# Identity products written into the modelled waits of a hybrid two-layer step

## The chip, the cores and the metric

The kernel runs on one core of one Trainium2 chip. The metric is the device time of one execution in microseconds (us); the kernel before takes 2547.45 us, the median of 3 runs (2543.54 to 2550.54).

## The reference

One step of a streaming encoder with two layers. 512 new frames of one prompt stream and 16 frames of each of 8 running streams go through it: 640 rows of width 2048, as five token blocks of 128 rows. All arithmetic is in fp32.

```
for i in range(DEPTH):                      # 2 layers
    shift, scale, gate = split(c @ w_ada[i] + b_ada[i], 3)
    h = rmsnorm(x, norm_g[i]) * (1 + scale) + shift
    if i % 2 == 0:                          # layer 0: stick-breaking attention
        q, k, v, zg = split(h @ w_in, 4)    # 16 heads of 128
        A = exp(log_sigmoid(z) - sum of softplus(z) over the keys between)   # z = q k / sqrt(128)
        y = ((A @ v) * silu(zg)) @ w_out
    else:                                   # layer 1: gated linear attention (GLA)
        q, k, v, r, a = split(h @ w_in)     # 4 heads, 256 x 512 state
        S = exp(b_last) * S + (k * exp(b_last - b))^T v     # chunk by chunk
        y = (rmsnorm(o) * silu(r)) @ w_out
    x = x + gate * y
y = rmsnorm(x, final_norm_g)
```

The running streams also bring 512 cached keys and values each, and a GLA state that is read, updated and written.

## The kernel before, in words

**Stages.** The program is one stream of work, in this order on the span: a front stage of layer 0 (about 0 to 160 us: x is turned, the conditioning products with w_ada give shift and scale, and the first 512 columns of the input projection are made), the rest of the input projection, the attention of layer 0 together with its output projection (about 950 to 1500), the front of layer 1, its input projection with GLA beside it, the output projection of layer 1 and the final norm. Weights come from DRAM in pieces, are cast into a high and a low part (`wh`, `wl`, L134 on ScalarE (ACT) and L135 on VectorE (DVE)), and each product of the projections is three matmuls (high by high, high by low, low by high).

**TensorE's order.** The whole kernel runs with TensorE (PE) on a written order: PE executes its matmuls as the Python code issues them. The order of the other engines is made by a scheduler that simulates a timeline, save in a few stretches with a written order there too (a stretch from the end of the front stage of layer 0 on, and most of the front of layer 1). The Python code itself is a planner. It keeps a modelled clock, `pe["now"]`, which `by` moves on for each matmul (a high or low part of n columns: n/2400 + 0.0133 us; fp32: n/600 + 0.005 us; narrow ones by another rule) and `block` by 0.11 us for a 128-column transpose. The main matmuls are generators. Everything else that needs PE is a "lane", another generator, held by an object of class `Side`. A lane says with each `step` how long to wait on the modelled clock and which PSUM banks it will take. `tick` runs what is due, and `drive` runs main matmuls with a `tick` between them.

**Modelled waits.** At some places the main matmuls can't go on before a lane has come to some point (six in the front stage of layer 0 through `ready`, the groups of the output projections, the end of a stage through `finish`). There the planner calls `Side.until(done)`: while `done()` is false it calls `tick`, and if that ran nothing, it moves the modelled clock by 0.2 us. In before, such a step of 0.2 us emits nothing. It is a wait of the model alone; whether the chip waits at that place is decided by the semaphores of the instructions around it.

**What stands around those places.** In the front stage of layer 0 the lane `ada_mod` gets pieces `ar` of w_ada by DMA, 512 KB each for the earlier steps, and multiplies them with `cT` (L180, a product of 32 columns of weights in one of four column tiles, into the bank `z` or `tp`); L185 on DVE copies the sum to `ada_r`, L189 turns it by two identity products, and from it come shift and scale, and then the activations `h`. The main matmuls there are L516 (`six`: five banks `mm`, 512 columns of the projection for all tokens), 512 columns wide. After the stage come L592 (products of 320 columns). At the end of the attention stage PE turns cached keys (L1079, an identity product in fp32), makes scores of cached keys (L1093, L1098), the values (L1131), turns probabilities (L1116, L1117) and runs the output projection of layer 0 (L696). In the front of layer 1 the rows are turned (L1306, whose copy is ACT's L1308), L248 spreads the norm over all partitions by a product of `rstd_w` and the identity in fp32, and L516 again makes 512 columns. At the end of the GLA, L1853 multiplies the running streams' states `s`, which GpSimd's queue loads (`move`, L78), L1859 makes the new states' updates, L1591 turns outputs, L1628 makes decays, and L696 is now the output projection of layer 1.

**PSUM.** There are eight banks of 128 x 512 fp32. `share_banks` opens pools by tag: in both front stages 5 `mm`, 1 `z` and 2 `tp`; elsewhere other splits. `bank(tag)` hands out the next buffer of a tag; a write to it waits until the earlier user of the buffer has been read.

Of the kernel before, what the change touches and what calls it, by code (L numbers as in the profile page):

```python
# [8 lines left out]
F32 = mybir.dt.float32  # L9
# [6 lines left out]
P = 128  # L16
# [25 lines left out]
def hybrid_step_kernel(ctx: ExitStack, tc: tile.TileContext, A: dict, O: list):  # L42
# [9 lines left out]
    mm, turn_block = nc.tensor.matmul, nc.tensor.transpose  # L52
# [37 lines left out]

    psum = {}

    def share_banks(**bufs):

        banks.close()
        psum["pool"] = banks.enter_context(tc.tile_pool(name="ps", bufs=1, space=PS))
        psum["bufs"] = bufs

    def bank(tag):
        return psum["pool"].tile([P, 512], F32, tag=tag, name=f"ps_{tag}", bufs=psum["bufs"][tag])  # L100

    share_banks(mm=5, z=1, tp=2)


    ident = cp.tile([P, P], F32, name="ident")
# [55 lines left out]
    def ada_mod(pool, ring, i, j0, ns, tag, group, pace=None, close=None):  # L161
# [5 lines left out]
        for kt in range(0, KT, each * group):  # L167
            rs = []
            for k in range(kt, kt + each * group, each):
                r = ring()  # L170
                for e in range(each):
                    load(r[:, 4 * w * e:4 * w * e + 4 * w].rearrange("p (q m) -> p q m", q=2),
                         src[:, k + e, 0:2, 256 * j0:256 * j0 + 2 * w])
                rs.append(r.rearrange("p (e q c) -> p e q c", e=each, q=4))
            yield step(pace(group) if pace else 0.5, tiled=True)
            if acc is None:
                acc = bank(tag)
            for m in range(each * group):
                for q in range(4):
                    mm(acc[32 * q:32 * q + 32, :w], cT[:, kt + m, :], by(cT[:, kt + m, :], rs[m // each][:, m % each, q, :]),  # L180
                       start=kt + m == 0, stop=kt + m == KT - 1)
# [3 lines left out]
        dve.tensor_copy(row, acc[:, :w])  # L185
        yield step(1.5, tp=1)
        tp = bank("tp")
        for s in range(ns):
            turn_block(tp[:, P * s:P * s + P], block(row[:, P * s:P * s + P]), ident)  # L189
# [87 lines left out]
    class Side:  # L277
# [56 lines left out]

        def until(self, done):

            while not done():
                if not self.tick():
                    pe["now"] += 0.2

        def finish(self):
            self.until(lambda: not self.lanes and not self.due)
# [42 lines left out]
    class Quarters:  # L385
# [89 lines left out]
        def again(self, i, pool):  # L475

            for n in range(0, 8, 3):
# [4 lines left out]
                for e in range(w):  # L482
                    self.upper[n + e] = slot(8 + n + e, (P, 2, HALF))
                    halves(self.upper[n + e][:, 0], self.upper[n + e][:, 1], r[:, e])

    def six(h, w, n0, acc, until, asked, first=0):


# [263 lines left out]
    with tc.tile_pool(name="st", bufs=1, reuse_waits="tile") as st:  # L752
# [21 lines left out]
        for a in range(TOK):  # L774
            ss4 = st.tile([P, 4], F32, tag="ss4", name="ss4", bufs=2)
            for q in range(4):
# [3 lines left out]
                tp = bank("mm")  # L780
# [8 lines left out]
            if a == 2:  # L789
                tp = bank("tp")  # L790
# [112 lines left out]


    share_banks(mm=2, z=2, tp=4)
    side.share(tp=4, z=2)
    og0 = {}
    w_out0 = A["sb_w_out"][0]
    with tc.tile_pool(name="kp", bufs=2, reuse_waits="tile") as kp, \
# [306 lines left out]
        first = [wraw(w_out0.rearrange("(kt p) n -> p kt n", p=P)[:, n:n + 2, :512], 2, 512) for n in (12, 14)]  # L1216
        side.finish()
        ring3["pool"] = None
    share_banks(mm=5, z=1, tp=2)
    side.share(tp=2, z=1)  # L1220


# [4 lines left out]
    with tc.tile_pool(name="o0", bufs=1, reuse_waits="tile") as po, ExitStack() as only_d:  # L1227
# [3 lines left out]
        t = sp.tile([P, 1280], F32, tag="s2", name="c1")  # L1231
# [3 lines left out]
        t = sp.tile([P, 512], F32R, tag="s7", name="middles")  # L1235
# [114 lines left out]

        acc = [bank("mm") for _ in range(5)]
        gemm = six(h2, w_in1, 2 * NK, acc, until, lambda: None, 2)
        next(gemm)
        for n in range(8):
# [37 lines left out]
        for kt in range(KT):  # L1392
            for nt in range(2):
                for n, x in enumerate(h2.part(kt, nt)):
                    mm(low[nt][:32, :HALF], wa[:, kt, :], by(wa[:, kt, :], x), start=kt == 0 and n == 0,
                       stop=kt == KT - 1 and n == 1)
# [59 lines left out]
        n = 0  # L1456
# [37 lines left out]
    with tc.tile_pool(name="gl", bufs=1, reuse_waits="tile") as gl:  # L1494
# [30 lines left out]
        t = mask_g[1].rearrange("p (b t) -> p b t", b=NB)  # L1525
# [400 lines left out]
    with tc.tile_pool(name="o1", bufs=1, reuse_waits="tile") as po:  # L1926
# [3 lines left out]
        for kt in range(10, 16):  # L1930
            r = po.tile([P, T], F32, tag="rows", name="og_in", bufs=6)
            load(r, og_d[kt // 4][:, kt % 4, :])
            n = 20 + 2 * kt % 12
# [88 lines left out]
```

## Time and profile before

| | |
|---|---|
| median of 3 runs | 2547.45 us |
| the profiled execution | 2556.43 us, its span 2554.7 us |
| mean granted PE clock | 0.979 of full speed |
| PE busy | 2442.0 us, 96% of the span |
| DVE busy | 1582.3 us, 62% |
| ACT busy | 995.3 us, 39% |
| moved by DMA | 503.13 MB, 197 GB/s on average |

The profiled execution is 9.0 us (0.35%) longer than the median of the runs. PE records come twice: PE is the matmul, PEld the load of its weights, which lies beside the matmul before it. A matmul in fp32 has two records of each kind: where the order of the program has 32 products of L180, the trace has 64 records. Matmuls are pipelined, so the time that one costs is the distance between starts, not its own length. The granted clock (PEclk) is 1.00 at full speed; a stretch at half speed shows 0.50.

### The profile page before, as it was taken

The numbers are of one execution on the slowest core, as the hardware profiler recorded it, in microseconds if no ns is written. First come the engines' busy times: TensorE is split into PE (matmuls) and PEld (weight loads), VectorE is DVE, ScalarE is ACT, GpSimd is POOL, SyncE is SP. The second block draws the span as 40 slices with busy tenths as digits, with TensorE's granted clock in tenths as the row PEclk, the third lists the DMA queues.
The fourth block names the chain that finished last, engine by engine and source line by source line (L and its number), as shares of the span: only waits on it lengthen the run. The fifth ranks groups of instructions, "written<-read, shape, count | busy, mean of one in ns | idle before, by whom it ended". The sixth has DMA issues, their size and how long they took to land.

```text
span 2554.7 us, 43975 instructions
## 1 busy us (share of the span) xinstructions
PE 2442.0 (96%) x17561; PEld 2159.4 (85%) x17561; DVE 1582.3 (62%) x2565; ACT 995.3 (39%) x1730; POOL 164.1 (6%) x390
## 2 busy tenths in 40 slices
PE   6899999999999989999999989999999999979998
PEld 4589999998999989788887767999999988857776
DVE  5575555555666656666775677666766465555456
ACT  4332222222223334555442354333333464455223
POOL 0010000000000000000000000000000233243100
PEclk8899999999999999999999989999999999989999
DMA  9966666766654357778764753344444677785634
GB/s 341 321 211 210 223 212 201 239 215 196 220 186 122 118 188 236 248 245 253 255 211 123 232 184 114 105 121 139 118 115 117 209 230 244 228 283 191 210 117 147
DMA packets 469439, 503.13 MB, mean 197 GB/s; under 512 B 42730, under 2 KB 366450, under 8 KB 469106
## 3 DMA queue, kind: packets, MB, share of 16 engines
q1 hardware_dynamic: 446274, 436.60, 54.4%
q0 software_dynamic: 16048, 51.92, 6.1%
q10 hardware_dynamic: 6912, 11.80, 1.2%
q8 instruction: 138, 2.26, 0.4%
q14 instruction: 67, 0.55, 0.1%
HBM read 411.10 MB, written 89.13 MB: 196 GB/s over the span
## 4 chain that ended last, share of the span: by engine, by line
PE 77%; DMA 7%; DVE 5%; ACT 3%; issue 2%; POOL 0%; SPq 0%; ACTq 0%; POOLq 0%; DVEq 0%
PE ps_mm L592 39%; PE ps_mm L696 10%; PE ps_mm L650 7%; PE ps_mm L367 3%; PE ps_tp L1079 2%; PE ps_tp L1544 2%; DMA gv<-kr 1%; PE ps_mm L516 1%; PE ps_tp L1131 1%; PE ps_tp L1039 1%; PE ps_z L1015 1%; PE ps_z L180 1%; PE ps_mm L1993 1%; PE ps_z L1093 1%; PE ps_z L222 1%
## 5 line engine op out<-in xcount | busy, mean ns | idle before, releaser
L592 PE MATMUL ps_mm<-sums,wh 128*128 128x320 f32 x2752 | 616.5, 313 | 3.8 <-ACT wh L134 3.8
L592 PEld LDWEIGHTS ps_mm<-sums,wh 128*128 128x128 f32 x2752 | 460.8, 189 | 12.9 <-issue 7.4
L592 PE MATMUL ps_mm<-h,wh 128*128 128x320 f32 x2064 | 462.1, 312 | 2.1 <-DVE u L598 2.1
L592 PE MATMUL ps_mm<-sums,wl 128*128 128x320 f32 x1376 | 427.5, 311 | 1.1 <-DVE wl L135 1.1
L135 DVE TENSOR_TENSOR wl<-wr,wh 128x1024 fp32r<-128x1024 f32 x194 | 237.4, 1224 | 245.0 <-ACT wh L134 244.3
L592 PEld LDWEIGHTS ps_mm<-h,wh 128*128 128x128 f32 x2064 | 343.7, 188 | 17.7 <-issue 13.9
L134 ACT CAST wh<-wb 128x1024 fp32r<-128x1024 f32 x170 | 178.4, 1049 | 424.5 <-PE ps_mm L592 363.8
L134 ACT CAST wh<-wr 128x1024 fp32r<-128x1024 f32 x194 | 203.6, 1050 | 356.1 <-PE ps_mm L592 187.9
L592 PE MATMUL ps_mm<-h,wl 128*128 128x320 f32 x1032 | 319.3, 309 | 0.0
L650 PE MATMUL ps_mm<-h,wh 128*128 128x320 f32 x1152 | 268.8, 321 | 10.2 <-ACT wh L134 5.8
L592 PEld LDWEIGHTS ps_mm<-sums,wl 128*128 128x128 f32 x1376 | 259.8, 189 | 1.7 <-DVE wl L135 1.7
L135 DVE TENSOR_TENSOR wl<-wb,wh 128x1024 fp32r<-128x1024 f32 x170 | 207.9, 1223 | 59.6 <-ACT wh L134 59.3
L650 PEld LDWEIGHTS ps_mm<-h,wh 128*128 128x128 f32 x1152 | 195.6, 192 | 27.2 <-issue 12.3
L696 PE MATMUL ps_mm<-wh,ogh 128*128 128x512 f32 x460 | 201.5, 438 | 5.0 <-DVE y L701 4.0
L592 PEld LDWEIGHTS ps_mm<-h,wl 128*128 128x128 f32 x1032 | 194.0, 188 | 0.0
L696 PE MATMUL ps_mm<-wh,ogl 128*128 128x512 f32 x460 | 181.8, 395 | 0.3 <-DVE ogl L135 0.3
L696 PE MATMUL ps_mm<-wl,ogh 128*128 128x512 f32 x460 | 181.6, 395 | 0.0
L650 PE MATMUL ps_mm<-h,wl 128*128 128x320 f32 x576 | 180.2, 313 | 0.4 <-DVE wl L135 0.4
L696 PEld LDWEIGHTS ps_mm<-wh,ogh 128*128 128x128 f32 x460 | 87.2, 189 | 33.5 <-issue 18.7
L650 PEld LDWEIGHTS ps_mm<-h,wl 128*128 128x128 f32 x576 | 110.1, 191 | 0.8 <-DVE wl L135 0.8
L696 PEld LDWEIGHTS ps_mm<-wh,ogl 128*128 128x128 f32 x460 | 87.0, 189 | 20.6 <-DVE ogl L135 0.7
L516 PE MATMUL ps_mm<-wh,h 128*128 128x512 f32 x252 | 93.5, 433 | 4.3 <-ACT h L134 1.9
(355 smaller groups left out, 3736.0 us busy)
## 6 DMA issues: line engine op xcount, KB each, us to landing
ar<-in_w_ada_dram SPq DMA_DIRECT2D x160, 512.0 KB
wb<-in_sb_w_in_dram SPq DMA_DIRECT2D x82, 512.0 KB
kc<-in_cache_sb_k_dram SPq DMA_DIRECT2D x64, 512.0 KB
vc<-in_cache_sb_v_dram SPq DMA_DIRECT2D x64, 512.0 KB
wr<-in_gla_w_in_dram SPq DMA_DIRECT2D x51, 512.0 KB
wb<-in_gla_w_in_dram SPq DMA_DIRECT2D x45, 512.0 KB
wr<-in_sb_w_in_dram SPq DMA_DIRECT2D x44, 512.0 KB
ar<-in_w_ada_dram SPq DMA_DIRECT2D x64, 256.0 KB
```

The lines of the kernel that those rows point to most:

```text
L134: nc.scalar.copy(hi, x)
L135: (e or dve).tensor_tensor(lo, x, hi.bitcast(F32), op=ALU.subtract)
L180: mm(acc[32 * q:32 * q + 32, :w], cT[:, kt + m, :], by(cT[:, kt + m, :], rs[m // each][:, m % each, q, :]), start=kt + m == 0, stop=kt + m ...
L222: mm(acc[32 * j:32 * j + 32, :256], cT[:, kt + m, :], by(cT[:, kt + m, :], r[:, 256 * j:256 * j + 256]), start=kt + m == 0, stop=kt + m == ...
L367: mm(acc[a], l[:, c], by(l[:, c], r[:, k2, :]), start=kt == k0 and first, stop=kt == k0 + nk - 1 and last)
L516: mm(acc[a], l, by(l, r[:, e, :]), start=j == 0 and e == 0 and begun, stop=j == 7 and e == 1 and last)
L592: mm(acc, l[:, k, :], by(l[:, k, :], r), start=start and k == 0 and first, stop=k == 7 and last, skip_group_check=True)
L650: mm(acc[nt], l[:, k, :], by(l[:, k, :], r), start=k0 == 8 and k == 0 and first, stop=k0 == 0 and k == 7 and last)
L696: mm(acc, l, by(l, r[:, e, :]), start=i == 0 and e == 0 and first, stop=i == 1 and e == 1 and last)
L1015: mm(z[:, :n], q[:, hh, qs], by(q[:, hh, qs], k[:, hh, :n]), start=True, stop=True)
L1079: turn_block(tp[:, P * c:P * c + P], block(kc[:, c, P * hh:P * hh + P]), ident)
L1544: mm(out, l[a], by(l[a], r[b]), start=start and n == 0, stop=stop and n == 2, skip_group_check=True)
```

## The change

`share_banks` takes a tag `spare`, and `bank` remembers the last tile of each tag. A new function `keep_on` issues one fp32 matmul: the identity (128 x 128) as weights, its first 72 columns as the moving operand, into columns 384 to 455 of a bank. Where `spare` is "z" (both front stages) the bank is the `z` tile that was handed out last, of which the other users take the columns below 384, and the matmul neither starts nor ends a sum. Elsewhere `keep_on` takes a fresh `mm` bank, once per call of `until`, and each of its matmuls starts and ends a sum of its own. Nobody reads those columns. `until` calls `keep_on` for each modelled wait of 0.2 us, and the modelled clock isn't moved by it, so that the planner's order of all other PE instructions is as before. Line numbers grow by 12 behind `share_banks` and by 14 behind `until`; the new matmuls are L111 of the kernel after.

```
-    def share_banks(**bufs):
+    def share_banks(spare="mm", **bufs):
 
         banks.close()
         psum["pool"] = banks.enter_context(tc.tile_pool(name="ps", bufs=1, space=PS))
         psum["bufs"] = bufs
+        psum["spare"], psum["at"] = spare, {}
 
     def bank(tag):
-        return psum["pool"].tile([P, 512], F32, tag=tag, name=f"ps_{tag}", bufs=psum["bufs"][tag])
-
-    share_banks(mm=5, z=1, tp=2)
+        t = psum["at"][tag] = psum["pool"].tile([P, 512], F32, tag=tag, name=f"ps_{tag}", bufs=psum["bufs"][tag])
+        return t
+
+    def keep_on(out=None, n=72):
+
+        own = psum["spare"] != "z"
+        if own and out is None:
+            out = bank(psum["spare"])
+        if not own:
+            out = psum["at"]["z"]
+        mm(out[:, 384:384 + n], ident, ident[:, :n], start=own, stop=own, skip_group_check=True)
+        return out
+
+    share_banks(spare="z", mm=5, z=1, tp=2)
...
         def until(self, done):
 
+            out = None
             while not done():
                 if not self.tick():
                     pe["now"] += 0.2
+                    out = keep_on(out)
...
-    share_banks(mm=5, z=1, tp=2)
+    share_banks(spare="z", mm=5, z=1, tp=2)
     side.share(tp=2, z=1)
```

In all, 277 such matmuls stand in PE's order, in 38 groups: 166 in the front stage of layer 0 (17 groups, into `z`), 28 at the end of the attention stage (7, into `mm`), 32 in the front of layer 1 (5, into `z`), 36 towards the end of the GLA, ahead of the first group of its output projection that has to wait (6, into `mm`), and 15 ahead of a later group (3, into `mm`). Four of them wait themselves: those that come first after a reader of their bank, three for DVE (two ahead of the turnings L189 and one in the front of layer 1) and one for ACT. These waits are ones that the next instruction of PE had before, or stand just ahead of it.

PE's order in the front stage of layer 0, where the third step of the conditioning ends (trace of before: 71.85 to 81.85 us). `ps_z` and `ps_tp` are the banks `z` and `tp`, x16 says that 16 such rows follow one another. Before:

```order
L180 MATMUL ps_z<-ar,cT 32x256 x32
L189 MATMUL ps_tp<-ident,ada_r 128x128 x2
L180 MATMUL ps_tp<-ar,cT 32x256 x16
L516 MATMUL ps_mm<-wh,h 128x512
L516 MATMUL ps_mm<-wl,h 128x512
```

The same place on PE after the change, where L192 is the L180 of before, L201 is L189 and L530 is L516:

```order
L192 MATMUL ps_z<-ar,cT 32x256 x16
L111 MATMUL ps_z<-ident 128x72 x23
L192 MATMUL ps_z<-ar,cT 32x256 x16
L111 MATMUL ps_z<-ident 128x72 x8
L201 MATMUL ps_tp<-ident,ada_r 128x128 x2
L192 MATMUL ps_tp<-ar,cT 32x256 x16
L111 MATMUL ps_z<-ident 128x72 x28
L530 MATMUL ps_mm<-wh,h 128x512
L530 MATMUL ps_mm<-wl,h 128x512
```

Nothing has changed places: 59 identity products have come in, 23 in the middle of a sum, 8 ahead of the turning and 28 ahead of the projection's products.

PE's order towards the end of the GLA (2264.67 to 2270.84 us in the trace of before), from the state updates to the products with the states `s`. Before:

```order
L1859 MATMUL ps_tp<-vst,kst_20583 128x512 x4
L1591 MATMUL ps_tp<-ident,on 128x128 x4
L1628 MATMUL ps_tp<-alr_in,wa_22805 128x320 x2
L696 MATMUL ps_mm<-wh,ogh 128x512
L696 MATMUL ps_mm<-wl,ogh 128x512
L696 MATMUL ps_mm<-wh,ogl 128x512
L1853 MATMUL ps_z<-s_23409,qz_20582 32x512
```

PE's order there after the change, from the last of those four state updates on (L1873 is the L1859 of before, L1605 is L1591, L1642 is L1628, L710 is L696, L1867 is L1853; the buffers' numbers count on):

```order
L1873 MATMUL ps_tp<-vst,kst_20810 128x512
L111 MATMUL ps_mm<-ident 128x72 x15
L1605 MATMUL ps_tp<-ident,on 128x128 x4
L111 MATMUL ps_mm<-ident 128x72 x6
L1642 MATMUL ps_tp<-alr_in,wa_23032 128x320 x2
L111 MATMUL ps_mm<-ident 128x72 x9
L710 MATMUL ps_mm<-wh,ogh 128x512
L710 MATMUL ps_mm<-wl,ogh 128x512
L710 MATMUL ps_mm<-wh,ogl 128x512
L1867 MATMUL ps_z<-s_23636,qz_20809 32x512
```

Here 30 products stand between the updates and the output projection, and 2 more between each two of the four updates.

The other engines' instructions are the same ones, but the scheduler that orders them sees the new matmuls, and so some change places: in the front stage of layer 0 loads of `wr` (weights of the projection) pass two to six loads of `ar` on SyncE's (SP's) queue at three places; a few casts on ACT and DVE change places in both front stages and at the ends of the attention and of the GLA. GpSimd's queue (POOL) towards the end of the GLA, before, where `out_dram<-s` stores a new state, `og_93<-gate` stores outputs, and `s` loads a state:

```order
L78 DMA out_dram<-s_23301 128x512
L78 DMA out_dram<-s_23385 128x512
L78 DMA og_93<-gate 512x1x128
L78 DMA s_23508<-in_state_gla_dram 128x512
L78 DMA s_23510<-in_state_gla_dram 128x512
```

GpSimd's queue at the same place after:

```order
L78 DMA out_dram<-s_23528 128x512
L78 DMA out_dram<-s_23612 128x512
L78 DMA s_23772<-in_state_gla_dram 128x512
L78 DMA og_93<-gate 512x1x128
L78 DMA s_23774<-in_state_gla_dram 128x512
```

The first of these loads of a state now stands ahead of the store of `og`. The loads behind it in this part of the queue stand as before or, further on, behind loads of `vst` and stores that they were ahead of.

## The prediction

> **What bounds the kernel now.** I read the page first, then the chain that ended last, then the waits and the clock stage by stage.
>
> ```profile
> PE 2442.0 (96%) x17561; PEld 2159.4 (85%) x17561; DVE 1582.3 (62%) x2565; ACT 995.3 (39%) x1730; POOL 164.1 (6%) x390
> PE   6899999999999989999999989999999999979998
> PE 77%; DMA 7%; DVE 5%; ACT 3%; issue 2%; POOL 0%; SPq 0%; ACTq 0%; POOLq 0%; DVEq 0%
> ```
>
> The first row is busy time, the second PE's busy tenths in 40 slices of 64 us, the third the shares of the chain that ended last. PE is busy for 96% of the span and is 77% of the chain. Work that is added to PE is therefore free only where PE waits, or where it buys clock. So the question is where the 277 new products fall. The planner put them where its own clock had nothing to run; the trace tells whether the chip has nothing to run there. For the front stage of layer 0, with 166 of them, these are all of PE's waits from the first product to the stage's end (total, times, longest in us):
>
> ```profile
> PE ps_tp L180 <- DMA ar<-in_w_ada_dram: 9.1, 11, 2.8
> PE ps_z L180 <- DMA ar<-in_w_ada_dram: 4.2, 9, 1.6
> PE ps_tp L248 <- DVE rstd_w L243: 2.5, 1, 2.5
> PE ps_tp L189 <- DVE ada_r L185: 1.8, 3, 0.9
> PE ps_mm L592 <- ACT wh L134: 1.5, 1, 1.5
> PE ps_mm L516 <- DVE h L135: 1.0, 2, 0.6
> PE ps_mm L516 <- ACT h L134: 0.8, 2, 0.4
> PE ps_mm L592 <- DVE wl L135: 0.7, 1, 0.7
> ```
>
> L248's wait is over before the first new product, which leaves 19.1 us in many short pieces, 13.3 us of them for pieces `ar` of w_ada. The other thing that can be won there is the clock (stretch, its length, busy times, then PEclk, DMA share and GB/s):
>
> ```profile
> 45.00:56.00 11.00, 8.90 (x78) 5.37 (x79) 3.39 (x6) 2.34 (x4) 0.00 (x0) 0.58 1.07 395
> 56.00:80.00 24.00, 21.13 (x199) 12.96 (x201) 13.50 (x36) 7.98 (x13) 0.00 (x0) 1.00 0.99 369
> 80.00:95.00 15.00, 13.35 (x72) 7.40 (x68) 12.45 (x29) 6.93 (x14) 0.00 (x0) 0.66 1.05 398
> 115.00:123.00 8.00, 7.21 (x47) 4.30 (x48) 4.62 (x10) 3.39 (x6) 0.00 (x0) 0.57 1.09 382
> ```
>
> Three stretches run at little over half clock, and the DMA engines are full (shares about 1.0) in all of them.
>
> **The price of one product.** No row of before has 128 columns of weights with 72 moving ones. The nearest are identity products in fp32 with 128 moving columns, two records each (start, length in us):
>
> ```profile
> 28.86 0.49 PE L248 MATMUL ps_tp<-ident,rstd_w 128*128 128x128 f32 x2 [2.54 <-DVE rstd_w L243]
> 28.86 0.30 PEld L248 LDWEIGHTS ps_tp<-ident,rstd_w 128*128 128x128 f32 x2 [2.78 <-DVE rstd_w L243]
> L248 PEld LDWEIGHTS ps_tp<-ident,rstd_w x20: 186/190/338, 9.4 to 1498.1; 128*128 128x128 f32 x20
> L1015 PE MATMUL ps_z<-k,q x128: 270/432/596, 945.6 to 1359.4; 128*128 128x128 f32 x32, 128*128 128x256 f32 x32, 128*128 128x384 f32 x32, 128*128 128x512 f32 x32
> 1058.56 1.04 PE L1079 MATMUL ps_tp<-ident,kc 128*128 128x128 f32 x8
> ```
>
> The eight records of L1079 take 1.04 us from the first start to the last end; one alone of this shape is 0.27 long (L1015's shortest), so seven steps take 0.77 us, 0.11 us per record. Is that the moving side or the weights? After L248's wait nothing is in PE's way, and its two weight loads together take 0.30 us where one is 0.190: the second begins 0.11 us after the first, although hardly anything moves yet. So a load of 128 columns alone takes about 0.11 us, and fewer moving columns don't shorten it: 2 x 0.11 = 0.22 us per new product. The other end: L1015's shortest record (128 columns) has 270 ns and its longest (512) 596, so a moving column adds (596 - 270)/384 = 0.85 ns, and 72 take 61 ns; if only the moving side counted, 2 x 0.061 = 0.12 us. I take 0.22, as both rows have the same weights in the same form. All 277 are then 61 us (33 us at 0.12).
>
> **Front stage of layer 0: 166 x 0.22 = 36.5 us.** If every one of the 19.1 us of waits absorbs its part, 17.4 us are left. From these goes what a clock at full speed wins back:
>
> ```profile
> 71.85 3.23 PE L180 MATMUL ps_z<-ar,cT 128*32 128x256 f32 x56
> 75.44 0.64 PE L180 MATMUL ps_z<-ar,cT 128*32 128x256 f32 x8 [0.35 <-DMA ar<-in_w_ada_dram]
> ...
> 81.85 0.79 PE L516 MATMUL ps_mm<-wh,h 128*128 128x512 f32 x1
> ...
> 89.02 3.24 PE L180 MATMUL ps_tp<-ar,cT 128*32 128x256 f32 x32
> 92.19 0.50 PE L516 MATMUL ps_mm<-wh,h 128*128 128x512 f32 x1
> ...
> 95.77 0.39 PE L516 MATMUL ps_mm<-wh,h 128*128 128x512 f32 x1
> 95.99 0.40 PE L516 MATMUL ps_mm<-wl,h 128*128 128x512 f32 x1
> ```
>
> At full clock L516 steps by 95.99 - 95.77 = 0.22 to 0.23 us. From 81.85 to 89.02 there are 12 of its products and some 1 us of its waits for `h` (the table's 1.0 and 0.8 are for the whole stage): 6.2 us instead of 2.7. The 32 L180 behind them take 3.2 us; at 71.85 the step was (75.44 - 0.35 - 71.85)/56 = 0.058, which makes 1.9. That stretch wins 4.7 us. The other two have lost, by their clock and PE's busy time, 0.42 x 8.9 = 3.7 and 0.43 x 7.2 = 3.1 us; I take 2 of the first, about half of which is L180 that waits for DMA in any case, and 2.8 of the second: 9.5 us together. The stage ends 36.5 - 19.1 - 9.5 = **7.9 us later**. The place that makes it: the 23, 8 and 28 products of the fence on PE's order cost 59 x 0.22 = 13 us between 71.85 and 81.85, and in all 24 us from 56 to 80 PE is idle for only 24 - 21.13 = 2.9 us. Below, the end is 36.5 - 19.1 - 11.3 if the clock is counted from the windows (0.42 x 8.9 + 0.34 x 13.4 + 0.43 x 7.2 = 11.3 us), about 6; above, where the waits for L592's casts and half of the short ones move along, some 14. The loads of `wr` that pass `ar` on SP's queue bring as many bytes in another order and are taken at nothing: the DMA engines are full either way, and what covers this is the delay of PE itself. Where it fails, an `ar` is late by up to its six 512 KB or so at 400 GB/s, at most the few us between these ends. Behind the stage PE's tenths are 9 in each slice from 128 to 896 us and 8 in the next, so PE makes its own time there and the delay stays.
>
> **End of the attention: 28 x 0.22 = 6.2 us.**
>
> ```profile
> 1064.55 1.09 PE L1079 MATMUL ps_tp<-ident,kc 128*128 128x128 f32 x8 [1.24 <-DMA kc<-in_cache_sb_k_dram]
> 1066.04 1.06 PE L1079 MATMUL ps_tp<-ident,kc 128*128 128x128 f32 x8 [0.40 <-DVE kt L1081]
> 1071.00:1076.00 5.00, 4.71 (x70) 2.92 (x69) 1.89 (x5) 1.28 (x4) 0.00 (x0) 0.66 0.82 295
> ```
>
> The two waits absorb 1.6 us, a full clock from 1071 to 1076 wins up to 0.34 x 4.7 = 1.6: **3 us later**, between 2 and 5.
>
> **Front of layer 1: 32 x 0.22 = 7.0 us.**
>
> ```profile
> 1495.47 1.11 PE L1306 MATMUL ps_tp<-ident,y 128*128 128x128 f32 x4 [3.66 <-ACT xp L1308]
> 1498.01 0.77 PE L248 MATMUL ps_tp<-ident,rstd_w 128*128 128x128 f32 x2 [1.43 <-DVE rstd_w L243]
> 1499.86 0.80 PE L516 MATMUL ps_mm<-wh,h 128*128 128x512 f32 x1 [1.08 <-ACT h L134]
> ```
>
> The groups of 15, 6 and 3 (3.3, 1.3 and 0.7 us) stand ahead of these three waits and fit. The groups of 2 and 6 (1.8 us) stand further ahead, in front of an earlier L248, and delay through the norm what ACT and DVE do: **1 us later** (0.4 to 1.8).
>
> **End of the GLA: 36 x 0.22 = 7.9 us, then 15 x 0.22 = 3.3 us.**
>
> ```profile
> 2280.70 0.56 POOL L78 DMA_DIRECT2D s<-in_state_gla_dram  x1 [3.67 <-issue]
> 2285.19 1.92 PE L1853 MATMUL ps_z<-s,qz 128*32 128x512 f32 x2 [12.42 <-DMA s<-in_state_gla_dram]
> 2373.13 0.40 PE L696 MATMUL ps_mm<-wh,ogh 128*128 128x512 f32 x1
> ```
>
> The 36 lie ahead of a wait of 12.42 us for a state, which covers them whole unless the state comes earlier. It does move up by one place, but POOL issued it only 3.67 us after the `og` store was out, with nothing else to do, so its queue was full; I give it 1 us of the wait: **1 us sooner**, with 3 us either way, since new states' stores ahead of it wait for products behind the new ones. At 2372 PE has no wait: **3.3 us later** (1.8 at 0.12).
>
> **Sum:** 7.9 + 3 + 1 - 1 + 3.3 = 14.2 us on the profiled 2556.4 (0.55%). That execution is 9.0 us above the median of the runs, so on the median: 2547.45 + 14 = **2561.5 us**. Differences under 0.3% (7.6 us) are what a measurement of this kernel can hardly tell from none.
>
> **Rivals.**
>
> *No change: the weights cost nothing extra.* If a product costs its moving columns (0.12 us), the front stage gets 19.9 us, against 19.1 of waits and 9.5 of clock, of which at that price not all are reachable, since a PE that is warm waits longer for DMA: about 0. The attention's end gives 3.4 - 1.6 - 1.6 = 0, the GLA's 1.8 - 1, the front of layer 1 about 0.5: +1.5 us, 2549 (2544 to 2554). For it: it is the planner's own price. Against it: the second weight load of L248. The Trainium skill's page "TensorE: Matmul & The Clock Gate", section "Back-to-back issue gap", gives N/2.4 + 2.5 ns for an isolated matmul with N moving columns, weights left out; taken for 4 x 72 columns that is an estimate of 0.12 to 0.13 us, this rival's price, and by it the kernel would take this rival's 2549.
>
> *Faster: the clock pays for more than the products.* The mechanism is the front stage alone: PE there is held by DMA, every wait absorbs its part, and the clock's 9.5 us come on top. It decides from a price below (19.1 + 9.5)/166 = 0.17 us per product; at 0.12 the stage ends 8.7 us sooner and the kernel at 2547.5 - 8.7 = 2539. Against it: the 59 products ahead of 81.85 are far more than the waits there, so their excess can't be absorbed by waits at 36 to 50 us.
>
> *Slower by far: no clock won.* If the stretches at half clock have another cause than the short waits, or sparse products (61 of 110 ns moving) don't hold the clock, the 9.5 + 1.6 us stay lost: 2547.5 + 14 + 11 = 2572 or more, since a product at half clock costs more (L248's longest weight load is 338 ns). Against it: 80 to 95 us runs at 0.66 although PE was busy for 21.13 of the 24 us ahead of it and the longest wait of the whole stage is 2.8, so short waits do cost clock. For it speaks a rule: the Trainium skill, on that page, section "Why this matters for your kernels", has the clock fall at idle gaps of more than about 3 us between bursts, and by that alone no wait of this stage would have cost clock, nor its filling win any. By that rule the kernel comes to this rival's 2572; the trace doesn't agree with it here, with 0.66 behind waits of at most 2.8 us.
>
> *The change does nothing* can't be: the products are in PE's order and PE isn't skipped.
>
> **How the numbers follow.** Forecast 0.56 (2553 to 2570), no change 0.22, faster by the clock 0.14, far slower 0.08. Slower by over 0.3% (above 2555.1): all of the far slower case and 0.52 of the forecast's, 0.60. Faster (below 2539.8): 0.14 and little of the others, 0.15. The rest, 0.25, is within. The range leaves out most of the faster case and half of the far slower: 2541 to 2571.
>
> **What would show it.** Right: L111 in rows at 0.21 to 0.22 us each, more busy PE by some 60 us less the clock's part, PEclk near 1.00 in 80 to 95, L592's first product some 8 us later, the wait at 2285 down by 8. Wrong: L111 at 0.12, waits for `ar` as long as before, or PEclk below 0.8 in the front stage.

## The result, and the profile after

The changed kernel takes 2567.59 us (median of 15 runs, 2560.03 to 2574.98). The kernel before, run beside it 15 times in all, takes 2552.09 us (2543.54 to 2560.80). The ratio is 1.0058, 95% interval 1.0045 to 1.0071: slower by 0.58%, 12 to 18 us. The forecast was 14 us.

The profiled execution of the changed kernel took 2563.17 us, 4 us less than its median, and that of before 2556.43, 4 us more than its median over 15 runs. The two traces are therefore only 6.8 us apart in span, and a comparison has to go stretch by stretch. From the page after (span; busy times; the clock in tenths over 40 slices; the chain):

```profile
span 2561.5 us, 45094 instructions
...
PE 2488.3 (97%) x18115; PEld 2226.1 (87%) x18115; DVE 1583.1 (62%) x2565; ACT 994.9 (39%) x1730; POOL 164.6 (6%) x390
...
PEclk8999999999999999999999989999999999999999
...
PE 85%; DMA 6%; DVE 4%; ACT 3%; issue 2%; POOL 1%; SPq 0%; ACTq 0%; POOLq 0%; DVEq 0%
```

PE has 554 more records, two for each of the 277 products, and its share of the chain has grown from 77 to 85%: work has taken the place of waits. The new line by itself, from its row (duration in ns, least, median and largest):

```profile
L111 PEld LDWEIGHTS ps_z<-ident x396: 186/192/338, 29.1 to 1517.1; 128*128 128x128 f32 x198
L111 PE MATMUL ps_z<-ident x396: 223/275/489, 29.1 to 1517.3; 128*128 128x72 f32 x198
```

The largest durations are the half clock's. What PE still waits for in the front stage of layer 0, 29 to 175 us, is all in two rows:

```profile
PE ps_z L111 <- DVE ada_r L197: 1.0, 2, 0.5
PE ps_mm L606 <- DVE wl L147: 0.7, 1, 0.7
```

Before, it was 19.1 us behind the first product, and the waits for the pieces `ar` are gone altogether: PE comes to each of them too late to wait. So the new order of the loads can't have held PE up in this stage. The place that the prediction had singled out, in the timeline after (start, length, engine, line; L192 is the L180 of before, L530 is L516):

```profile
87.19 2.00 PE L111 MATMUL ps_z<-ident 128*128 128x72 f32 x16 [0.55 <-DVE ada_r L197]
89.03 0.38 PE L201 MATMUL ps_tp<-ident,ada_r 128*128 128x128 f32 x2
89.35 1.93 PE L192 MATMUL ps_tp<-ar,cT 128*32 128x256 f32 x32
91.21 6.47 PE L111 MATMUL ps_z<-ident 128*128 128x72 f32 x56
97.48 0.48 PE L530 MATMUL ps_mm<-wh,h 128*128 128x512 f32 x1
```

The 28 products take 97.48 - 91.21 = 6.27 us, 0.224 each, at full clock. The projection's product that began at 81.85 begins at 97.48, 15.6 us later, where it was 5.7 later at 71.85 before the groups of 23, 8 and 28. The clock in the stretches (stretch, length, busy times, then PEclk, DMA share and GB/s):

```profile
29.00:45.00 16.00, 15.59 (x171) 13.20 (x163) 3.01 (x13) 0.14 (x1) 0.00 (x0) 0.50 1.00 333
45.00:56.00 11.00, 11.00 (x158) 9.40 (x150) 6.39 (x15) 4.35 (x8) 0.00 (x0) 0.94 1.06 393
80.00:95.00 15.00, 14.45 (x159) 12.29 (x158) 5.97 (x19) 4.21 (x10) 0.00 (x0) 1.00 1.02 371
115.00:123.00 8.00, 8.00 (x106) 6.31 (x105) 4.86 (x13) 2.95 (x6) 0.00 (x0) 1.00 0.69 216
```

The three stretches at half clock of before are at 0.94 and 1.00. But half clock now comes earlier: from 29 to 45 us PE is busy for 15.59 of 16 us and still runs at 0.50, where before it had 0.75:

```profile
29.00:45.00 16.00, 10.38 (x199) 6.63 (x203) 7.57 (x22) 2.78 (x6) 0.00 (x0) 0.75 0.93 306
```

At the end of the attention the largest group (12 products) stands where before nothing stood between two lines, and nothing waits there:

```profile
1069.07 2.80 PE L111 MATMUL ps_mm<-ident 128*128 128x72 f32 x24
1071.79 1.07 PE L1107 MATMUL ps_z<-kt,q_one 128*32 128x256 f32 x16
```

In the front of layer 1 the products run at half clock (timeline, then the window's row):

```profile
1503.32 2.50 PE L111 MATMUL ps_z<-ident 128*128 128x72 f32 x12 [4.73 <-DVE ss L1328]
1505.61 0.73 PE L260 MATMUL ps_tp<-ident,rstd_w 128*128 128x128 f32 x2
1506.13 6.51 PE L111 MATMUL ps_z<-ident 128*128 128x72 f32 x30
1512.44 1.06 PE L1320 MATMUL ps_tp<-ident,y 128*128 128x128 f32 x4
1513.29 2.67 PE L111 MATMUL ps_z<-ident 128*128 128x72 f32 x12
1515.76 0.73 PE L260 MATMUL ps_tp<-ident,rstd_w 128*128 128x128 f32 x2
```

```profile
1507.00:1520.00 13.00, 13.00 (x57) 12.52 (x57) 9.45 (x23) 7.59 (x19) 0.00 (x0) 0.50 0.30 110
```

The 15 products take 1512.44 - 1506.13 = 6.3 us, 0.42 each, and fill more than the wait of 3.66 us that was there. A second delay stands in the first row: the first product of the group of 6 waits 4.73 us for DVE, which reads its bank only then, and with it waits the turning product L260 behind it. Before, this was an L248 that waited for nothing:

```profile
1491.42 0.39 PE L248 MATMUL ps_tp<-ident,rstd_w 128*128 128x128 f32 x2
```

So here, other than the section on the change says of such waits, the next instruction of PE did not have this one. Counted from the same product of L696 (1489.04 us before, 1495.65 here), the first L530 of the stage starts 10.95 us later than its L516 did, by the wait and by the price together. Behind it much of that is won back: until 1600 us PE waits 2.8 us there, where before it waited 7.7.

At the end of the GLA (PE, and below it GpSimd's queue):

```profile
2271.50 3.46 PE L111 MATMUL ps_mm<-ident 128*128 128x72 f32 x30
...
2288.38 1.91 PE L1867 MATMUL ps_z<-s,qz 128*32 128x512 f32 x2 [7.65 <-DMA s<-in_state_gla_dram]
...
2377.04 2.57 PE L111 MATMUL ps_mm<-ident 128*128 128x72 f32 x22
2379.41 0.48 PE L710 MATMUL ps_mm<-wh,ogh 128*128 128x512 f32 x1
```

```profile
2282.26 0.54 POOL L78 DMA_DIRECT2D s<-in_state_gla_dram  x1 [2.69 <-issue]
2284.85 0.72 POOL L78 DMA_DIRECT2D og<-gate  x1 [2.04 <-issue]
```

The wait for the state has shrunk from 12.42 to 7.65 us, and its load now goes out ahead of the `og` store. Counted from the same PE instruction (2264.09 us before, 2268.65 here), the load goes out 3.0 us sooner, PE comes to the wait 3.4 us later, and the wait ends 1.4 us sooner. The 11 products at 2377 take 2.4 us with no wait near.

To weigh each place against the scatter between executions, I measured in every trace of this study the time between the starts of the same two PE instructions, named by their time in the trace of before. "Without" is the mean (and the ends) over the kernels that have no new products in that stretch; the kernels of the other columns are those of the experiments below.

| stretch (time in before) | without | the change | only front of layer 0 | all but front of layer 0 | only front of layer 1 |
|---|---|---|---|---|---|
| start to 163 us | 161.7 (159.8 to 163.2, 4 kernels) | 171.7 | 173.1 | | |
| 1057 to 1078 | 19.9 (19.1 to 21.3, 8) | 22.1 | | 22.0 | |
| 1489 to 1600 | 109.8 (108.4 to 111.0, 7) | 113.3 | | 114.8 | 113.8 |
| 2264 to 2291 | 26.9 (25.6 to 27.8, 7) | 25.1 | | 24.7 | |
| 2370 to 2380 | 10.0 (10.0 to 10.0, 8) | 13.6 | | 13.4 | |

The change's terms by this table: +10.0, +2.2, +3.5, -1.8 and +3.6, together 17.5 us, at the upper end of the measured 12 to 18. Stretches without any product differ by some us between kernels (the second column), so the sum can't be had much closer from one trace per kernel, and the -1.8 is little more than that scatter.

### The profile page after: what moved, and what is told of

Read it like the earlier page. It is cut to its first block, busy times and chain, and to the rows that moved or that the text cites. A ratio compares the mean times of both kernels' runs of the same rounds, so it can differ in the third digit from the quotient of the medians.

```text
span 2561.5 us, 45094 instructions
## 1 busy us (share of the span) xinstructions
PE 2488.3 (97%) x18115; PEld 2226.1 (87%) x18115; DVE 1583.1 (62%) x2565; ACT 994.9 (39%) x1730; POOL 164.6 (6%) x390
## 4 chain that ended last, share of the span: by engine, by line
PE 85%; DMA 6%; DVE 4%; ACT 3%; issue 2%; POOL 1%; SPq 0%; ACTq 0%; POOLq 0%; DVEq 0%
PE ps_mm L606 39%; PE ps_mm L710 11%; PE ps_mm L664 7%; PE ps_mm L530 4%; PE ps_mm L381 3%; PE ps_tp L1093 2%; PE ps_z L111 2%; PE ps_z L192 2%; PE ps_tp L1558 2%; DMA gv<-kr 1%; PE ps_tp L1145 1%; PE ps_tp L1053 1%; PE ps_z L1029 1%; PE ps_z L1107 1%; PE ps_mm L2007 1%
## 5 line engine op out<-in xcount | busy, mean ns | idle before, releaser
L710 PE MATMUL ps_mm<-wh,ogh 128*128 128x512 f32 x460 | 201.0, 437 | 4.3 <-DVE y L715 2.9
L710 PE MATMUL ps_mm<-wh,ogl 128*128 128x512 f32 x460 | 181.1, 394 | 0.2 <-DVE ogl L147 0.2
L710 PE MATMUL ps_mm<-wl,ogh 128*128 128x512 f32 x460 | 180.9, 393 | 0.0
L710 PEld LDWEIGHTS ps_mm<-wh,ogh 128*128 128x128 f32 x460 | 87.0, 189 | 32.5 <-issue 16.6
L710 PEld LDWEIGHTS ps_mm<-wh,ogl 128*128 128x128 f32 x460 | 86.6, 188 | 20.5 <-DVE ogl L147 0.6
L710 PEld LDWEIGHTS ps_mm<-wl,ogh 128*128 128x128 f32 x460 | 87.3, 190 | 11.1 <-issue 0.2
```

Of the source, the lines that this page charges most:

```text
L710: mm(acc, l, by(l, r[:, e, :]), start=i == 0 and e == 0 and first, stop=i == 1 and e == 1 and last)
```

## The experiments

Theory: a product takes PE for the load of its 128 weight columns, 0.22 us at full clock, and what exceeds the waits at its place delays everything behind it. Rival 1: a product costs its moving columns. Rival 2: the delay isn't PE's work, but the waits that the products carry and the new order of the other engines. Besides, how much the clock gives back was open. Each ratio is against the kernel before on the same chip, with its 95% interval.

**Eight columns instead of 72.**

```
-    def keep_on(out=None, n=72):
+    def keep_on(out=None, n=8):
```

> Each of the 277 products moves 8 columns instead of 72; weights, places and waits are as in the change. Theory (a product costs the load of its 128 weight columns, twice 0.11 us): the records stand 107 to 112 ns apart as with 72 columns, and the time is the changed kernel's, 1.0055 of the kernel before (1.004 to 1.007). Rival 1 (a product costs its moving columns): some 0.02 to 0.05 us each, the time is that of before or less, 0.997 to 1.001. Rival 2 (the delay is not PE's work but the waits that the products carry and the new order of the other engines): 1.0058 as well, with records closer together.

Measured: 2596.85 us, 1.0181 (1.0161 to 1.0200), far slower than all had it. Timeline and clock of this kernel:

```profile
90.59 6.02 PE L111 MATMUL ps_z<-ident 128*128 128x8 f32 x46
96.54 3.64 PE L192 MATMUL ps_z<-ar,cT 128*32 128x256 f32 x32
...
108.33 9.01 PE L111 MATMUL ps_z<-ident 128*128 128x8 f32 x56
117.19 0.77 PE L530 MATMUL ps_mm<-wh,h 128*128 128x512 f32 x1
```

```profile
29.00:45.00 16.00, 15.59 (x191) 13.22 (x179) 3.76 (x15) 0.47 (x2) 0.00 (x0) 0.54 0.96 321
45.00:56.00 11.00, 11.00 (x102) 10.18 (x98) 6.25 (x14) 3.98 (x8) 0.00 (x0) 0.50 0.91 321
115.00:123.00 8.00, 8.00 (x35) 6.32 (x39) 5.22 (x10) 1.35 (x2) 0.00 (x0) 0.54 0.00 2
```

The price isn't the moving columns': with a ninth of them the 23 products at 90.59 take 5.95 us, 0.26 each, and the 28 at 108.33 0.32, where the change took 0.23 and 0.22. At full clock the records are 112 ns apart, as with 72 columns; at half clock 213. So the weight load sets the price, and rival 1 is out. What the theory had missed is the clock: this kernel fills the same waits, PE is busy without a gap, and the clock stays at half over long stretches. The start to 163 us takes 200.6 us here.

**32 weight columns instead of 128.**

```
-        mm(out[:, 384:384 + n], ident, ident[:, :n], ...)
+        mm(out[:32, 384:384 + n], ident[:, :32], ident[:, :n], ...)
```

> Each of the 277 products has 32 columns of the identity as weights instead of 128, and 72 moving columns as in the change. Theory (load of 128 columns): the load falls to about a quarter (0.03 us), the moving side is left with 61 ns a record, a product costs 0.12 us, and the time is near that of before: 1.0005 (0.998 to 1.003). Rival 1 (moving columns set the 0.22 us): unchanged, 1.0055. Rival 2 (waits and order): unchanged, 1.0058.

Measured: 2557.78 us, 1.0023 (1.0012 to 1.0034). The group of 28 of this kernel:

```profile
83.17 3.66 PE L111 MATMUL ps_z<-ident 128*32 128x72 f32 x56
86.76 0.50 PE L530 MATMUL ps_mm<-wh,h 128*128 128x512 f32 x1
```

28 products in 3.59 us, 0.128 each: close to the 0.12 that the prediction worked out for the moving side alone. On PE the places and the number are the change's, and the time lost has fallen to less than half (the order on the other engines is not wholly the change's: 6 places on SP's queue and 56 of DVE's 2565 instructions differ). Rival 2, which had the time unchanged, is out for most of the change. In the front of layer 1 the group of 6 waits for DVE here too (4.9 us), and yet that stretch takes 109.8 us, as without any product.

The Trainium skill, page "TensorE: Matmul & The Clock Gate", section "LDWEIGHTS (loading the stationary operand)", puts a load at its number of columns over 1.2 in ns. This case agrees at full clock: by that rule an estimate for 128 columns is 107 ns, and the records stood 112 ns apart whether 8, 72 or 128 columns moved.

**Only the front stage of layer 0, and all but it.** `until` calls `keep_on` in that stage alone, or everywhere else alone.

```
         psum["spare"], psum["at"] = spare, {}
+        psum["first"] = "first" not in psum
...
+                    if psum["first"]:        # in the other kernel: if not psum["first"]
                         out = keep_on(out)
```

> Only the 166 products of the front stage of layer 0 are written, the other 111 are left out. Theory: the stage ends 8 to 9 us later and the kernel takes 1.0034 of before (1.002 to 1.005). Rival 2 (waits carried by the products in the front of layer 1, and GpSimd's new order at the end of the GLA): next to nothing is left, 1.000.

> The 166 products of the front stage of layer 0 are left out, the other 111 are written. Theory: 3 at the end of the attention, 1 to 2 in the front of layer 1, -1 to -2 and +3 at the end of the GLA: 5 to 6 us, 1.0022 (1.001 to 1.0035). Rival 2 (waits in the front of layer 1 and GpSimd's order): most of the change's 1.0058 is here, 1.005.

Measured: 2565.22 us, 1.0057 (1.0039 to 1.0074), and 2560.97 us, 1.0031 (1.0019 to 1.0043). Both parts cost, the front stage the most, as the theory has it; rival 2 had nearly all in the second. The two together are 0.88%, more than the change's 0.58%; the intervals (0.21 either way for the sum, 0.13 for the change) and the scatter of a kernel with nothing changed (below) make up nearly all of that difference, and I can't say whether anything is left.

**Only the front of layer 1.**

```
         psum["spare"], psum["at"] = spare, {}
+        psum["k"] = psum.get("k", 0) + 1
...
+                    if psum["k"] == 3:
                         out = keep_on(out)
```

> Only the 32 products of the front of layer 1 are written. The prediction's step gives 1 us (0.4 to 1.8), 1.0005. In the trace of the changed kernel they run at half clock, 0.38 to 0.42 us each, and the first group waits 5 us for DVE ahead of L248: if that isn't taken in by the slack behind, up to 5 us, 1.002.

Measured: 2558.21 us, 1.0027 (1.0015 to 1.0039). The stretch from 1489 to 1600 takes 113.8 us instead of 109.8: 4 us, not 1; the rest of the 0.27% (7 us) is not placed. The wait of the group of 6 isn't enough by itself, since it stands with 32 weight columns as well and costs nothing there. But no run has the products with 128 weight columns without the wait, so the price isn't shown to be enough either. Counted from 1489.04, the first product of the projection starts 4.0 us later than before with 32 weight columns and 11.3 us later here, and behind it 4 to 7 us are taken up again. Wait (4.7 us) and price at half clock together exceed that; by this sum each alone would be taken up for the most part.

**Every second product left out.**

```
+                    psum["n"] = psum.get("n", 0) + 1
+                    if psum["n"] % 2 == 0:
                         out = keep_on(out)
```

> Every second of the 277 products is left out, each group keeps its place: 138 products, 83 in the front stage of layer 0. Theory (PE's time for the products beyond the waits at their places): 31 us of products instead of 62; in the front stage 18.6 us against 19.1 of waits and 9.5 of clock, of which the groups ahead of the projection can't reach all, so the stage ends within 3 us of before; 1.001 in all (0.998 to 1.003). The rival that the clock pays for more than the products once they are cheap enough: 0.996. If half as many products don't hold the clock: 1.003 or more.

Measured: 2557.80 us, 1.0034 (1.0022 to 1.0046). Half of the products cost about half (0.34 of 0.58%), and that is more than the theory had, 1.001 and at most 1.003 (the interval reaches below that end). The rival that the clock pays for more than the products, once they are cheap enough, is out: it had 0.996. The start to 163 us takes 166.3 us, 4.6 more than without, where the theory had at most 3. That half as many products don't hold the clock (1.003 or more) fits the ratio, but the trace shows it in one stretch alone: 0.76 from 45 to 56 us, and 0.95, 1.00 and 1.00 in the other three shown above. Where the excess comes from stays open.

**Products in the real waits.** No product in the modelled waits; in the front stage of layer 0, ahead of those pieces `ar` for which PE waited in the trace of before, as many as fit the wait: 51 with 128 weight columns, then 98 with 32 (the two expectations say 50 and 95; the traces have 102 and 196 records, two for each).

```
+FILL = {18: 4, 19: 1, 20: 1, 21: 1, 22: 12, 26: 9, 47: 1, 48: 1, 49: 2, 50: 3, 51: 2,
+        69: 2, 70: 1, 71: 7, 73: 1, 74: 1, 75: 2}
...
             for m in range(each * group):
+                psum["piece"] = psum.get("piece", -1) + 1
+                for _ in range(FILL.get(psum["piece"], 0)):
+                    keep_on()
```

> No product in the modelled waits; instead 50 of the same products in the front stage of layer 0, right ahead of those pieces of the conditioning for which PE waited in the trace of before, as many as fit the wait at 0.22 us each. Theory: they cost nothing there; if they hold the clock, the 9.5 us at half clock are won and the kernel takes 0.9965 (0.995 to 0.999). If the clock falls all the same, 1.000 to 1.002, since a product then takes 0.43 us and no longer fits its wait.

> As the run before, with 32 columns of weights instead of 128 (0.126 us each) and 95 products, as many as fit the same waits. Theory: 0.9965 (0.995 to 0.999), with more room than before, as these products fill their time with moving columns; if the clock falls all the same, 1.000.

Measured: 2564.84 us, 1.0056 (1.0039 to 1.0074), and 2549.75 us, 0.9997 (0.9985 to 1.0009). The first missed by far. Timeline of that kernel, at the wait of 2.75 us that it should have filled:

```profile
42.26 5.40 PE L113 MATMUL ps_z<-ident 128*128 128x72 f32 x24
47.59 1.94 PE L197 MATMUL ps_tp<-ar,cT 128*32 128x128 f32 x32
```

The clock had fallen by then, and 12 products take 5.3 us, 0.44 each. With 32 weight columns (two windows of that kernel) the clock holds:

```profile
45.00:56.00 11.00, 9.54 (x120) 6.82 (x116) 3.53 (x8) 2.34 (x4) 0.00 (x0) 1.00 1.07 395
80.00:95.00 15.00, 12.34 (x74) 7.71 (x73) 11.88 (x28) 6.44 (x13) 0.00 (x0) 0.89 1.03 386
```

and the stage still ends only 1.8 us sooner than without products (159.9 against 161.7), which is within what the kernels without differ by (159.8 to 163.2). From the first product of the conditioning on, PE's other work took 102.4 us (114.4 before), but the products took 13.9 and the waits shrank only from 19.4 to 14.3 us. The DMA shares of 1.07 and 1.03 are the reason that the trace offers: a PE that is faster between two pieces only comes to the next piece sooner. It waits elsewhere, too; these are rows of its waits from 29 to 161 us:

```profile
PE ps_tp L206 <- DVE ada_r L202: 3.3, 4, 1.5
...
PE ps_mm L535 <- DVE h L149: 2.1, 2, 1.8
```

Both were shorter before (1.8 and 1.0 us).

**Of the 51, only the 23 behind 52 us.** `FILL` without its first six entries.

> Of the run with 50 products of 128 weight columns in the waits of the front stage, the 28 ahead of 50 us are left out, where the clock was at half in that run and a product took 0.43 us; 22 stay. If those 28 made that run slow (1.0056): 0.999 to 1.001. If it is the later ones or another order on other engines: 1.004 or more.

Measured: 2555.64 us, 1.0011 (0.9999 to 1.0023). So leaving out the first 28 takes back most of the 0.56% of the run with all 51. Not all of these 28 ran at half clock there, as the expectation has it: the first four stood 0.22 to 0.28 us apart, the 12 at 42.26 us 0.43, and of the 9 at 49.45 us all but the first 0.22. The two profiled executions differ by 7.4 us, and 6.3 of it are there at 163 us (165.1 and 158.8 us). Against the kernels without products, however, the run with all 51 was only 3.4 us longer up to 163 us, and what the rest of its 14 us is stays open: its trace has a wait of 4.3 us for DVE's `k` in the GLA, where the other traces have 1.0 to 3.0, in a place that this edit doesn't touch.

**Long waits too.** The 98 products, and 40, 42 and 80 more ahead of three long waits.

```
+    def fill_in(t, count):
+        for _ in range(count):
+            mm(t[:32, 384:456], ident[:, :32], ident[:, :72], start=True, stop=True, skip_group_check=True)
...
+                if psum["scores"] == 0:
+                    fill_in(z, 40)
...
+                        if psum["state"] in LONG:
+                            fill_in(bank("tp"), LONG[psum["state"]])
```

> The 95 products with 32 weight columns in the waits of the front stage, as before, and 40, 42 and 80 more ahead of three long waits further on (5.7 us for q_one at 955 us, 5.9 and 12.4 us for states at 2194 and 2285 us), into columns or banks that nobody reads. Theory: at 0.126 us they fit the waits (5.0, 5.3 and 10.1 us) and hold the clock, so that the half clock behind each of these waits (2 to 3 us each) is won: 0.9965 (0.994 to 0.999). If the clock behind the long waits isn't held, or the products delay what PE does for the next loads: 1.000 to 1.002.

Measured: 2548.02 us, 0.9989 (0.9979 to 0.9999). Its windows behind the waits:

```profile
955.00:975.00 20.00, 19.26 (x198) 17.86 (x191) 10.42 (x28) 8.70 (x23) 0.36 (x5) 1.00 0.85 268
...
2194.00:2215.00 21.00, 21.00 (x144) 20.57 (x144) 12.71 (x24) 10.81 (x24) 7.75 (x14) 1.00 0.89 235
```

The clock was 0.91 in both before and is 1.00 now:

```profile
955.00:975.00 20.00, 19.59 (x194) 17.65 (x195) 10.41 (x28) 7.94 (x21) 0.36 (x5) 0.91 0.83 261
2194.00:2215.00 21.00, 21.00 (x127) 19.23 (x126) 13.72 (x26) 12.14 (x23) 9.36 (x17) 0.91 0.80 231
```

The kernel is 0.1% faster (0.0 to 0.2), a third of what was expected.

**The changed code with no product at all.**

```
-                    out = keep_on(out)
+                    pass
```

> The changed kernel's code with keep_on never called: every engine's order is that of the kernel before. Both theories: 1.000; how far it comes out from that (0.9985 to 1.0015 expected) says how much of the excess of the other runs can be scatter.

Measured: 2554.74 us, 1.0009 (0.9998 to 1.0020). This is the scatter: about 0.1%, with the same instructions as before. The run with 98 products (0.9997) isn't clear of it. The one with the long waits (0.9989) is 0.1% below the kernel before and, on the same chip, 0.26% below this one (2548.02 against 2554.74 us), so that a small gain is likely and its size isn't settled.

**128 columns instead of 72.**

```
-    def keep_on(out=None, n=72):
+    def keep_on(out=None, n=128):
```

> Each of the 277 products moves 128 columns instead of 72, weights as in the change. Theory: the price stays that of the weight load, 0.22 us at full clock, but PE is now moving all the time within a product, so if moving columns hold the clock, the stretches from 29 to 46 us and in the front of layer 1 that ran at half clock in the changed kernel run faster: the time falls to 1.003 to 1.005. If moving columns don't matter for the clock at this density, 1.0058 as with 72. If moving columns set the price, 1.010 or more.

Measured: 2566.87 us, 1.0060 (1.0048 to 1.0073), no faster than the change, where the theory had 1.003 to 1.005. But the clock does hold in the front stage of layer 0, and is 0.81 instead of 0.50 in the front of layer 1:

```profile
29.00:45.00 16.00, 13.09 (x236) 10.42 (x234) 8.45 (x31) 4.76 (x10) 0.55 (x1) 1.00 0.92 301
45.00:56.00 11.00, 10.79 (x129) 9.05 (x126) 4.48 (x9) 2.34 (x4) 0.00 (x0) 1.00 1.07 396
...
1507.00:1520.00 13.00, 13.00 (x81) 12.35 (x80) 8.85 (x21) 7.05 (x17) 0.00 (x0) 0.81 0.51 161
```

and the records stay 112 ns apart, which is once more the weights' price. The start to 163 us takes 169.4 us instead of 171.7, and 1489 to 1600 112.1 instead of 113.3: by these two traces the clock's part is 2 and 1 us, and 3 us in 2560 are not seen in the ratio.

## Why the prediction was right, point by point

The time came out within the range and close to the forecast, 0.58% for 0.55%. The mechanism held: a price set by the weights, paid wherever the chip doesn't wait. That the number came out so close is luck in part, as two terms of the front stage were both too small by nearly the same amount. Step by step:

- **The price.** 0.22 us, right: 0.224 per product in the long groups at full clock. The argument from the second weight load of L248 holds, as 8, 72 and 128 moving columns have the same step and 32 weight columns about half of it. At half clock the price is 0.43, and that the forecast had only named, not counted.
- **Front stage of layer 0, +7.9 us.** Measured +10.0, with each half of the sum too small. The products' busy time, from the group's row of the changed kernel from 29 to 165 us,

```profile
L111 PE MATMUL ps_z<-ident 128*128 128x72 f32 x332 | 44.6, 294 | 1.0 <-DVE ada_r L197 1.0
```

  is 44.6 us; from start to start, which is what they cost, it is 42.4 and not 36.5, as the first 17 cost 0.43 to 0.50 each. The waits gave their 19.1 less 1.7, as taken. What is left, 42.4 - 17.4 - 10.0 = 15 us, was given back, and is more than 9.5: from the first product of the conditioning to 163 us, PE's other work took 114.4 us before and 99.5 after. The fuller clock is one part of that. Another is likely that work no longer cut up by waits is shorter: at a clock of 0.99 to 1.00 that work took 102.4 us in the run with 98 products in the real waits, where 14.3 us of waits were left, and 96.5 in the one with 128 moving columns, where 2.1 were left. No run separates the two for the change. The excess of the price, 5.9 us, and that of the gain, 5.5, nearly cancel, and that is the luck. That "every one of the waits absorbs its part" held.
- **End of the attention, +3 us:** +2.2. Right.
- **Front of layer 1, +1 us:** +3.5. Two steps failed. The groups of 15, 6 and 3 do not "fit" their waits: at 0.38 to 0.42 us each they are 6.3, 2.5 and 1.1 us for waits of 3.66, 1.43 and 1.08. And the other group of 6, put at its price alone, waits 4.73 us for DVE and holds L248 back. Which of the two the +3.5 hangs on isn't shown; the runs show that the wait with cheap products costs nothing.
- **End of the GLA, -1 and +3.3 us:** -1.8 and +3.6. The wait for the state covered the 36 products: it fell by 4.8 us. The load that moved up a place went out 3.0 us sooner, and the wait ended 1.4 us sooner.
- **The basis.** The median of before over 15 runs is 2552.09 us, 4.6 more than the three runs had. The forecast as a difference is untouched by that; as a time it is 6 us below the result, of which 4.6 are this.

One of the prediction's signs of being wrong did appear, PEclk below 0.8 in the front stage: 0.50 from 29 to 45 us. Of its signs of being right, L111 stood at 0.22 us at full clock, the clock was 1.00 from 80 to 95 us, L592's first product came 10.3 us later (8 were named), and the wait at 2285 fell by 4.8 us (8 were named).

Of the rivals, "no change" fell with its price. "Faster by the clock" had its point of 0.17 us per product; at 0.128 the kernel was still 0.23% slower, so its assumption that every wait can be reached at any price is wrong: with 32 weight columns PE still waits 5.8 us for `ar` in that stage, beside products at other places that find no wait. "Slower by far" was half true: with 72 columns the clock held in three stretches and failed in two, and with 8 it came to that rival's side of the forecast, and beyond.

The rule of the Trainium skill that was weighed there (page "TensorE: Matmul & The Clock Gate", section "Why this matters for your kernels": the clock falls at idle gaps of over about 3 us) doesn't explain these runs: with 8 columns PE was busy for 15.59 of 16 us at a clock of 0.54.

## What to carry to other kernels

Work that only fills a planner's modelled waits is charged in full wherever the chip has no wait at that place: read the waits from a trace, place by place, before putting anything into them, and price the filler from a row with the same weights, since a load of 128 weight columns costs as much with 8 moving columns as with 128 at the same clock. By these runs a filler for the clock should spend its time on moving columns, with few weight columns. And where a full clock only brings PE sooner to a transfer that isn't there yet, it is worth little, even when it costs nothing.

## What the runs showed of the hardware that was not expected

- A PE that is busy by its records isn't enough for the clock. From 29 to 45 us the granted clock was 0.54 with 8 moving columns on 128 weight columns, 0.50 with 72 and 1.00 with 128; with 32 weight columns and 72 moving ones, in real waits, it was 1.00 there and from 45 to 56. The same place varies between executions and kernels (0.85 from 29 to 45 us in the kernel with the front stage's products alone, 0.95 with every second one), so that one number alone says little. But the mean granted clock of the whole span sets the 8 columns apart in every execution: 0.969 to 0.971 in 4 with 8 columns, 0.980 to 0.989 in 15 with 72, 0.987 to 0.989 in 5 with 128. Why is not shown; that time spent on loading weights counts less for the clock than time spent on moving columns would fit.
- At half clock a weight load of 128 columns took twice as long, 213 ns from record to record instead of 112.
- Two records of products with 32 weight columns and 72 moving ones stood 63 ns apart at full clock, 0.126 to 0.128 us per product, near the 61 ns that the prediction worked out for 72 moving columns. No run has 32 weight columns with another number of moving ones, so that nothing but these was left to pay is likely, not shown.
